# Index scores of a sparse attention layer: f32 products over half the rows replaced by pairs of F32R products over all 128

## The chip, the cores and the metric

The kernel runs on one core of a Trainium2 chip. The metric is the device time of one execution in microseconds; the figure given for a kernel is the median of several executions. Engines are named as the profile names them: PE multiplies matrices (PEld is its weight load), DVE is VectorE, ACT is ScalarE, POOL is GpSimd and SP issues most transfers.

## What is computed

Two blocks of two layers each, over 256 tokens (272 with 16 learned ones in the second block). The change sits in the third layer, whose first half is an attention in which every token attends only to the 64 keys with the highest index score:

```
iqb = iq[:, s0:s0 + 128]                                   # 8 index heads of 64
sc = jax.nn.relu(jnp.einsum('bqhd,bsd->bqhs', iqb, ik).astype(jnp.float32))
score = jnp.einsum('bqhs,bqh->bqs', sc, iwb.astype(jnp.float32)) * IDX_SCALE
score = jnp.where(adm[None], score, NEG_INF)
_, idx = lax.top_k(score, topk)                            # topk = 64
```

`iq` has 8 heads of 64, `ik` has one key of 64 for all heads, `iw` a weight for each head. `iq`, `ik` and `iw` are columns of one large input product of the layer.

## The kernel before

Activations lie transposed, features on partitions and tokens along the row. A large product is done in two parts: `hilo` (L338 to L341) writes a rounded copy of an f32 tile in the type F32R on ACT and the remainder, also F32R, on DVE, and `mm3` adds three products of such parts in one PSUM bank. `Stream.emit` (L267 to L293) loads each piece of weights (128x1024), splits it the same way (ACT at L289, DVE at L290) and keeps eight pieces; `take` hands two pieces to a product and asks for later ones, so L289 of a new piece has to wait until PE has read the piece that stood in its buffer. `tiles2` (L608) takes two pieces and makes two output tiles in the two PSUM banks `pd`, each from 24 matmuls of 272 columns; the next `tiles2` needs both banks evicted.

In `layer_ab` the input product gives, in this order: the tile `zn` with the index key, head weights and gate input; the four tiles `ps` with the index queries; `pq`; then by `tiles2` the GLA keys (evicted at L1251 into `k_`), two pairs of attention keys `ak` and two pairs of attention queries `aq` (all four pairs evicted at L1261 into the tile `akq`), and the values. While PE makes these, DVE, ACT and PE also do `decays` (L1333 to L1354: exponentials and cumulative sums of the gate) and `select`.

`select` evicts the four tiles of queries into the first half of `akq` (L1364), copies the key to both halves of the partitions (`ik`), and then, for each of two blocks of 128 queries (`wd` = 144 and 272 keys), makes eight score tiles in the four banks `pw`: one f32 matmul for each head, over 64 rows, two heads beside each other on the two halves of the rows. ACT takes relu from PSUM into `rl` (L1381, two buffers), and DVE adds them up with the head weight (L1383, L1385). Then DVE finds the 64 largest by eight rounds of `max` and `match_replace` (L1389, L1390).

The program is written in this order, but a scheduler of the framework sets the order of each engine's queue when the kernel is built, from its own estimates of times and from the buffers that come free. At run time every engine works through its queue in that order.

Of the kernel before, what the change touches and what calls it, by code (L numbers as in the profile page):

```python
# [10 lines left out]
F32 = mybir.dt.float32  # L11
F32R = mybir.dt.float32r
AF = mybir.ActivationFunctionType
OP = mybir.AluOpType
# [4 lines left out]
SEQ = 256  # L19
META = 16  # L20
T2 = SEQ + META
# [285 lines left out]
HALVES = slice(0, 64), slice(64, 128)  # L307


class K:  # L310
# [898 lines left out]
    def layer_ab(self, xh, xl, x, g):  # L1209

        nc, tc = self.nc, self.tc
        with tc.tile_pool(name="ab", bufs=1) as lp, tc.tile_pool(name="ab2", bufs=2) as l2:
# [6 lines left out]
            mk = [tile([128, wd], f"sc{t}") for t, wd in ((0, 144), (1, 272))]  # L1219

            w = [self.st.take() for _ in range(2)]
            zn = self.psum("w")[:, :T2]
            ps = [self.psum(b)[:, :SEQ] for b in "ddww"]
# [8 lines left out]
            _, r = self.lead(([[(zn, True)], [(ps[0], True), (ps[1], True)]], w), rest, hx, lx, T2)  # L1232
# [2 lines left out]
            nc.vector.tensor_scalar(rq, r, -0.125, None, op0=OP.mult)  # L1235
            nz = tile([128, T2], "nz")
            nc.vector.tensor_tensor(nz, zn, r, op=OP.mult)
            akq, gs = self.ag("akq", F32), self.ag("gs", F32)
            aq, ak = akq[:, :4], akq[:, 4:]
            eb, en, ed, qg = [gs[:, 2 * n:2 * n + 2] for n in range(4)]  # L1240
            dec = self.decays(nz, eb, en, ed, lp)
            self.select(nz, ps, r, mk, aq, lp, l2)

            kg, kdt = lp.tile([128, 2, T2], F32, tag="bc", name="kg"), tile([128, 3, 256], "kdt")
            for j, p in enumerate(pq):
# [27 lines left out]
            with tc.tile_pool(name="dsa", bufs=2) as dp:  # L1273
# [25 lines left out]
                ps = [self.psum("w")[:, :T2] for _ in range(4)]  # L1299
# [57 lines left out]
    def select(self, nz, ps, r, mk, iq, gp, l2):  # L1357

        nc = self.nc
        ik = gp.tile([128, T2], F32, name="ik")  # L1360
        nc.gpsimd.tensor_copy(ik[0:64], nz[0:64])
        nc.gpsimd.tensor_copy(ik[64:128], nz[0:64])
        for j in range(4):
            nc.vector.tensor_tensor(iq[:, j, 16:], ps[j], r[:, 16:], op=OP.mult)  # L1364
        iw = gp.tile([128, 2, 8], F32, name="iw")
        p = self.psum("m")
        for t in range(2):
            nc.tensor.transpose(p[:, 8 * t:8 * t + 8], nz[64:72, 16 + 128 * t:144 + 128 * t], self.ident[64:72, 64:72])
        nc.vector.tensor_scalar(iw.rearrange("p a b -> p (a b)"), p[:, :16], 64 ** -0.5 * 8 ** -0.5, None,
                                op0=OP.mult)  # L1370
        for t, sc in enumerate(mk):
            wd = sc.shape[1]
            for h in range(8):

                if h % 2 == 0:
                    two = [self.psum("w")[:, :wd] for _ in range(2)]
                    for p, hs in zip(two, HALVES):
                        self.mm(p, iq[hs, h // 2, 16 + 128 * t:144 + 128 * t], ik[hs, :wd])
                p = two[h % 2]
                rl = l2.tile([128, T2], F32, tag="rl", name="rl")[:, :wd]  # L1380
                nc.scalar.activation(rl, p, AF.Relu)  # L1381
                if h == 0:
                    nc.vector.tensor_scalar(sc, rl, iw[:, t, 0:1], None, op0=OP.mult)  # L1383
                else:
                    nc.vector.scalar_tensor_tensor(sc, rl, iw[:, t, h:h + 1], sc, op0=OP.mult, op1=OP.add)  # L1385
            nc.vector.memset(sc[0:64, wd - 64:wd], -BIG)
            m8 = gp.tile([128, 8], F32, name=f"m8{t}")
            for _ in range(8):
                nc.vector.max(m8, sc)  # L1389
                nc.vector.match_replace(sc, m8, sc, -3e38)  # L1390
            nc.vector.tensor_scalar(sc, sc, -2e38, BIG, op0=OP.is_gt, op1=OP.mult)
# [524 lines left out]
```

## Time and profile before

| | |
|---|---|
| median of 3 runs | 986.51 us (984.84 to 987.99) |
| the profiled execution | 982.69 us, span 980.9 us |
| PE busy | 956.9 us, 98% of the span |
| DVE busy | 667.9 us, 68% |
| ACT busy | 515.9 us, 53% |
| POOL busy | 92.0 us, 9% |
| mean granted clock of PE | 0.992 |

The span is the time from the first to the last instruction of the program in the one execution that was profiled; 1.8 us of that execution lie outside it. PE's busy time is modelled at its end, so a matmul's listed duration is longer than the distance to the next one; where rates are needed, distances between starts are read.

### The profile page before, as it was taken

Reading aid. Unit: us, or ns where it says so; the run is one execution under the profiler, and the core shown is the slowest. Engines: PE = TensorE matmul, PEld = TensorE weight load, DVE = VectorE, ACT = ScalarE, POOL = GpSimd, SP = SyncE. Lnnn points to the kernel's source line nnn. Section 1 sums busy time; section 2 is a strip of 40 time slices with the busy share of each in tenths; the row PEclk is TensorE's granted clock in tenths of the full one; section 3 lists DMA queues with packets and bytes.
Section 4 is the critical chain, followed back from the end, with each engine's and each line's share of the span. In section 5 each row is a group of like instructions: output and inputs, shape, how many; then the busy total and the mean of one; then the engine's idle time right before and its main releaser. Section 6 shows DMA issues by size and latency. Waiting matters only on the chain.

```text
span 980.9 us, 19189 instructions
## 1 busy us (share of the span) xinstructions
PE 956.9 (98%) x7638; PEld 898.9 (92%) x7638; DVE 667.9 (68%) x1369; ACT 515.9 (53%) x933; POOL 92.0 (9%) x121
## 2 busy tenths in 40 slices
PE   7999999999999999999999999999999999999996
PEld 6999989999999898887999999989898889998985
DVE  6889577545554899984954555558987756757762
ACT  7646366444445568873734444445635435353442
POOL 1121010000001100001000000010211211005121
PEclk9999999999999999999999999989999999999999
DMA  9744437655554364421565555546354314634201
GB/s 330 269 158 146 141 125 263 203 184 172 177 192 150 122 219 136 156 80 45 175 217 191 173 173 192 190 145 231 108 178 147 119 45 131 234 130 130 88 1 44
DMA packets 46074, 154.65 MB, mean 158 GB/s; under 512 B 6424, under 2 KB 7968, under 8 KB 45856
## 3 DMA queue, kind: packets, MB, share of 16 engines
q1 hardware_dynamic: 45552, 152.85, 46.5%
q8 instruction: 60, 0.98, 0.4%
q10 hardware_dynamic: 432, 0.57, 0.2%
q14 instruction: 30, 0.25, 0.1%
HBM read 152.34 MB, written 2.70 MB: 158 GB/s over the span
## 4 chain that ended last, share of the span: by engine, by line
PE 93%; DVE 3%; ACT 1%; DMA 1%; issue 1%; POOL 1%; SPq 0%; POOLq 0%; DVEq 0%; ACTq 0%
PE pd L328 45%; PE pw L328 38%; PE pm L328 6%; DVE st L290 1%; PE pm L1140 1%; PE pm L1172 1%; DMA st<-in_c_v 1%; DMA x<-in_xT 1%; ACT pm L1126 0%; POOL rc L389 0%; DVE zz L1030 0%; PE pm L1528 0%; PE pm L1730 0%; DVE x L521 0%; PE pw L881 0%
## 5 line engine op out<-in xcount | busy, mean ns | idle before, releaser
L290 DVE TENSOR_TENSOR st<-st,st 128x1024 fp32r<-128x1024 f32 (+2 forms) x274 | 327.3, 1212 | 162.7 <-ACT st L289 162.0
L289 ACT ACTIVATE st<-st 128x1024 fp32r<-128x1024 f32 (+2 forms) x274 | 279.4, 1041 | 275.1 <-PE pd L328 140.9
L328 PE MATMUL pd<-xh,st 128*128 128x256 f32 (+1 forms) x1856 | 357.0, 287 | 8.3 <-ACT st L289 6.3
L328 PEld LDWEIGHTS pd<-xh,st 128*128 128x128 f32 x1856 | 293.4, 189 | 15.5 <-ACT st L289 6.3
L328 PE MATMUL pd<-xl,st 128*128 128x256 f32 (+1 forms) x928 | 263.9, 286 | 0.6 <-DVE xl L428 0.6
L328 PE MATMUL pw<-hh,st 128*128 128x256 f32 x1024 | 188.4, 283 | 0.0
L328 PEld LDWEIGHTS pd<-xl,st 128*128 128x128 f32 x928 | 175.7, 189 | 2.8 <-DVE xl L428 1.3
L328 PEld LDWEIGHTS pw<-hh,st 128*128 128x128 f32 x1024 | 161.1, 191 | 0.0
L328 PE MATMUL pw<-hl,st 128*128 128x256 f32 x512 | 144.6, 283 | 0.0
L328 PEld LDWEIGHTS pw<-hl,st 128*128 128x128 f32 x512 | 98.0, 191 | 0.0
L328 PE MATMUL pd<-akq,st 128*128 128x272 f32 (+1 forms) x384 | 78.0, 293 | 0.0
L328 PE MATMUL pw<-xh,st 128*128 128x256 f32 (+1 forms) x384 | 75.2, 286 | 0.0
L328 PEld LDWEIGHTS pd<-akq,st 128*128 128x128 f32 x384 | 61.0, 188 | 2.3 <-issue 1.9
L328 PEld LDWEIGHTS pw<-xh,st 128*128 128x128 f32 x384 | 61.3, 190 | 1.1 <-ACT xh L533 0.7
L328 PE MATMUL pd<-gs,st 128*128 128x272 f32 (+1 forms) x192 | 55.3, 288 | 0.0
L328 PE MATMUL pw<-xl,st 128*128 128x256 f32 (+1 forms) x192 | 54.1, 284 | 0.0
L389 POOL TENSOR_TENSOR rc<-rc,mhalf 128x2 f32<-128x2 f32 (+4 forms) x17 | 19.9, 1173 | 317.6 <-DVE rc L386 314.6
L328 PE MATMUL pw<-mh,st 128*128 128x256 f32 x256 | 48.7, 285 | 0.3 <-ACT mh L340 0.2
L328 PEld LDWEIGHTS pw<-mh,st 128*128 128x128 f32 x256 | 40.3, 190 | 1.7 <-ACT mh L340 0.6
L328 PEld LDWEIGHTS pd<-gs,st 128*128 128x128 f32 x192 | 36.2, 189 | 0.5 <-issue 0.4
L328 PEld LDWEIGHTS pw<-xl,st 128*128 128x128 f32 x192 | 36.3, 189 | 0.0
L328 PE MATMUL pw<-ml,st 128*128 128x256 f32 x128 | 36.1, 289 | 0.0
(457 smaller groups left out, 1321.6 us busy)
## 6 DMA issues: line engine op xcount, KB each, us to landing
st<-in_w SPq DMA_DIRECT2D x128, 512.0 KB, 4.5
st<-in_ab_in SPq DMA_DIRECT2D x32, 512.0 KB, 3.9
st<-in_cd_in SPq DMA_DIRECT2D x28, 512.0 KB, 4.3
st<-in_a_in SPq DMA_DIRECT2D x18, 512.0 KB, 7.0
st<-in_c_in SPq DMA_DIRECT2D x16, 512.0 KB, 4.7
st<-in_a_out SPq DMA_DIRECT2D x8, 512.0 KB, 4.7
st<-in_c_out SPq DMA_DIRECT2D x8, 512.0 KB, 4.1
st<-in_ab_out SPq DMA_DIRECT2D x8, 512.0 KB, 3.9
```

The costliest lines, as they stand in the source:

```text
L289: self.last = self.nc.scalar.activation(hi[:, p], raw[:, p], AF.Copy).ins
L290: self.nc.vector.tensor_tensor(lo[:, p], raw[:, p], hi[:, p].bitcast(F32), op=OP.subtract)
L328: self.pe = self.nc.tensor.matmul(out, lhsT, rhs, start=start, stop=stop, skip_group_check=True).ins
L389: nc.gpsimd.tensor_tensor(r, r, self.mhalf[:p, :n], op=OP.pow)
L1140: nc.tensor.transpose(tp[:, 128 * j:128 * j + 128], src, self.ident)
L1172: nc.tensor.transpose(ps[:b - a, 128 * j:128 * j + 128], x[:, a:b], self.ident)
```

## The change

`select` now splits the index key and the index queries into F32R parts. The key's rounded part `ikh` and remainder `ikl` both stand on both halves of the rows (L340, L341). Each head of the queries gets a tile of all 128 rows: its rounded part on the half where the head came out of the product (ACT, L1373), the remainder on the other half (DVE, L1374, from the f32 copy `iqf` of L1371). One matmul with `ikh` and one with `ikl` then add all four products of parts in one bank. The eight heads fill the whole tile `akq`, so `layer_ab` asks for that tile a second time, for `aq` and `ak`, after `select`: the buffer is the same one, and its first writer (L1263) waits for the last index matmul.

```
@@ layer_ab
-            akq, gs = self.ag("akq", F32), self.ag("gs", F32)
-            aq, ak = akq[:, :4], akq[:, 4:]
+            iq, gs = self.ag("akq", F32R), self.ag("gs", F32)
             eb, en, ed, qg = [gs[:, 2 * n:2 * n + 2] for n in range(4)]
             dec = self.decays(nz, eb, en, ed, lp)
-            self.select(nz, ps, r, mk, aq, lp, l2)
+            self.select(nz, ps, r, mk, iq, lp, l2)
+            akq = self.ag("akq", F32)
+            aq, ak = akq[:, :4], akq[:, 4:]
@@ select
+        ikh, ikl = gp.tile([128, T2], F32R, name="ikh"), gp.tile([128, T2], F32R, name="ikl")
+        self.hilo(ikh, ikl, ik)
         for j in range(4):
-            nc.vector.tensor_tensor(iq[:, j, 16:], ps[j], r[:, 16:], op=OP.mult)
+            q = l2.tile([128, T2], F32, tag=f"vf{j % 2}", name="iqf")[:, :SEQ]
+            nc.vector.tensor_tensor(q, ps[j], r[:, 16:], op=OP.mult)
+            for f, h in enumerate(HALVES):
+                nc.scalar.activation(iq[h, 2 * j + f, :SEQ], q[h], AF.Copy)
+                nc.vector.tensor_tensor(iq[HALVES[1 - f], 2 * j + f, :SEQ], q[h], iq[h, 2 * j + f, :SEQ].bitcast(F32),
+                                        op=OP.subtract)
...
             for h in range(8):
-
-                if h % 2 == 0:
-                    two = [self.psum("w")[:, :wd] for _ in range(2)]
-                    for p, hs in zip(two, HALVES):
-                        self.mm(p, iq[hs, h // 2, 16 + 128 * t:144 + 128 * t], ik[hs, :wd])
-                p = two[h % 2]
+                p = self.psum("w")[:, :wd]
+                self.mm(p, iq[:, h, 128 * t:128 * t + 128], ikh[:, :wd], True, False)
+                self.mm(p, iq[:, h, 128 * t:128 * t + 128], ikl[:, :wd], False, True)
```

The scheduler orders the queues anew. Three places show it. The first is PE's queue where the third pair of `tiles2` begins (`pd_8469` before, `pd_8510` now: the second pair of attention keys). Before, the index matmuls of the second block stand one or two at a time between the projection's:

```order
L328 MATMUL pd_8469<-xl_7723,st1_8310 128x272
L328 MATMUL pw_8264<-ik_8173,akq_8135 128x272
L328 MATMUL pd_8469<-xh_7722,st2_8311 128x272
L328 MATMUL pd_8469<-xh_7722,st1_8310 128x272
L328 MATMUL pd_8469<-xl_7723,st1_8310 128x272
L328 MATMUL pd_8469<-xh_7722,st2_8311 128x272
L328 MATMUL pd_8470<-xh_7722,st1_8316 128x272
L328 MATMUL pd_8470<-xl_7723,st1_8316 128x272
L328 MATMUL pd_8470<-xh_7722,st2_8317 128x272
L328 MATMUL pw_8265<-ik_8173,akq_8135 128x272
L328 MATMUL pw_8274<-ik_8173,akq_8135 128x272
```

Now all sixteen of the second block, and the last four of the first, stand in one row ahead of that pair (its end is shown; `pw_8276` is the first of them, and each needs the bank of the head four before it):

```order
L328 MATMUL pw_8294<-ikh_8176,akq_8135 128x272
L328 MATMUL pw_8294<-ikl_8177,akq_8135 128x272
L328 MATMUL pw_8300<-ikh_8176,akq_8135 128x272
L328 MATMUL pw_8300<-ikl_8177,akq_8135 128x272
L328 MATMUL pw_8306<-ikh_8176,akq_8135 128x272
L328 MATMUL pw_8306<-ikl_8177,akq_8135 128x272
L328 MATMUL pw_8312<-ikh_8176,akq_8135 128x272
L328 MATMUL pw_8312<-ikl_8177,akq_8135 128x272
L328 MATMUL pw_8318<-ikh_8176,akq_8135 128x272
L328 MATMUL pw_8318<-ikl_8177,akq_8135 128x272
L328 MATMUL pd_8510<-xh_7722,st1_8351 128x272
L328 MATMUL pd_8510<-xl_7723,st1_8351 128x272
```

What was strewn among the projections' matmuls is now one block between the second and the third of these pairs.

The second place is ACT's queue from the last weight piece before `select` on. Before (L1381 is relu, L1335 to L1343 belong to `decays`):

```order
L289 ACTIVATE st_8400<-st_8399 128x1024
L289 ACTIVATE st_8458<-st_8457 128x1024
L1381 ACTIVATE rl<-pw 128x144 x2
L1335 ACTIVATE gs<-gs 128x544
L1381 ACTIVATE rl<-pw 128x144 x2
L1336 ACT_TABLE_LOAD
L1336 ACTIVATE gs<-gs 128x544
L289 ACTIVATE st_8464<-st_8463 128x1024
L1381 ACTIVATE rl<-pw 128x144 x3
```

Now (L1389 is relu, L1337 to L1345 belong to `decays`, `st_8441`, `st_8499`, `st_8505` and `st_8563` are the pieces 8400, 8458, 8464 and 8522 of before):

```order
L289 ACTIVATE st_8441<-st_8440 128x1024
L1373 ACTIVATE akq<-iqf 64x256 x8
L340 ACTIVATE ikh<-ik 128x272
L289 ACTIVATE st_8499<-st_8498 128x1024
L289 ACTIVATE st_8505<-st_8504 128x1024
L1389 ACTIVATE rl<-pw 128x144 x2
L289 ACTIVATE st_8563<-st_8562 128x1024
L1337 ACTIVATE gs<-gs 128x544
L1389 ACTIVATE rl<-pw 128x144 x2
L1338 ACT_TABLE_LOAD
L1338 ACTIVATE gs<-gs 128x544
L1389 ACTIVATE rl<-pw 128x144
```

Nine copies came in, and two weight pieces that stood behind the first relus now stand ahead of them or among them.

The third place is DVE's queue around the first evictions of attention keys. Before, the first stands nine rows further ahead, among the first block's sums; the second stands here, ahead of the second block's first sum (`sc_7901` and `sc_7902` are the score tiles of the two blocks):

```order
L290 TENSOR_TENSOR st_8523<-st_8521,st_8522 128x1024
L1385 SCALAR_TENSOR_TENSOR sc_7901<-rl,iw,sc_7901 128x144 x2
L1261 TENSOR_TENSOR akq<-pd,r 128x272
L1386 MEMSET sc_7901 64x64
L1383 TENSOR_SCALAR sc_7902<-rl,iw 128x272
```

Now both stand behind the fifth sum of the second block:

```order
L1393 SCALAR_TENSOR_TENSOR sc_7902<-rl,iw,sc_7902 128x272
L1397 MAX m_8258<-sc_7901 128x8
L1393 SCALAR_TENSOR_TENSOR sc_7902<-rl,iw,sc_7902 128x272
L1398 MATCH_REPLACE sc_7901<-m_8258,sc_7901 128x144
L1393 SCALAR_TENSOR_TENSOR sc_7902<-rl,iw,sc_7902 128x272
L1263 TENSOR_TENSOR akq<-pd,r 128x272 x2
```

The two evictions free the `pd` banks that the third pair needs.

## Rows read from the trace of the kernel before

**Rows 1.** The page: engines (busy us, share, instructions), chain that ended last.

```profile
PE 956.9 (98%) x7638; PEld 898.9 (92%) x7638; DVE 667.9 (68%) x1369; ACT 515.9 (53%) x933; POOL 92.0 (9%) x121
...
PE 93%; DVE 3%; ACT 1%; DMA 1%; issue 1%; POOL 1%; SPq 0%; POOLq 0%; DVEq 0%; ACTq 0%
```

**Rows 2.** Busy time by window (us: PE, PEld, DVE, ACT, POOL, PEclk, DMA, GB/s).

```profile
678.00:712.00 34.00, 34.00 (x228) 28.43 (x227) 29.19 (x84) 18.40 (x32) 6.30 (x8) 1.00 0.42 147
```

**Rows 3.** Timeline of PE (start, us, what, count): index matmuls among projections; each leaves two records.

```profile
682.89 0.28 PE L328 MATMUL pd<-xl,st 128*128 128x272 f32 x1
683.10 0.51 PE L328 MATMUL pw<-ik,akq 64*128 64x144 f32 x2
683.54 0.52 PE L328 MATMUL pd<-xh,st 128*128 128x272 f32 x2
683.90 0.29 PE L328 MATMUL pd<-xl,st 128*128 128x272 f32 x1
...
694.25 0.73 PE L328 MATMUL pw<-ik,akq 64*128 64x272 f32 x4
694.90 0.40 PE L328 MATMUL pd<-xl,st 128*128 128x272 f32 x1
...
696.27 0.29 PE L328 MATMUL pd<-xh,st 128*128 128x272 f32 x1
696.49 0.72 PE L328 MATMUL pw<-ik,akq 64*128 64x272 f32 x2
697.14 0.39 PE L328 MATMUL pd<-xh,st 128*128 128x272 f32 x1
697.37 0.29 PE L328 MATMUL pd<-xl,st 128*128 128x272 f32 x1
```

**Rows 4.** Timeline of DVE in the same stretch (idle before in brackets).

```profile
680.50 1.23 DVE L290 TENSOR_TENSOR st<-st,st 128x1024 fp32r<-128x1024 f32 x1
681.64 0.50 DVE L1333 TENSOR_SCALAR gs<-pm,ab_s 128x272 f32<-128x272 f32 x1
683.97 0.44 DVE L1251 TENSOR_TENSOR k__8371<-pd,r 128x272 f32<-128x272 f32 x1 [1.84 <-PE pd L328]
...
693.23 1.73 DVE L1340 TENSOR_TENSOR_SCAN bc<-one,gs 128x16 f32<-128x16 f32 x10
...
702.51 0.49 DVE L1385 SCALAR_TENSOR_TENSOR sc<-rl,iw,sc 128x272 f32<-128x272 f32 x1
```

**Rows 5.** Timeline of ACT in the same stretch.

```profile
683.26 1.06 ACT L289 ACTIVATE st<-st 128x1024 fp32r<-128x1024 f32 x1 [2.79 <-PE pd L328]
...
688.38 0.48 ACT L1381 ACTIVATE rl<-pw 128x144 f32<-128x144 f32 x2
688.88 1.28 ACT L1336 ACT_TABLE_LOAD   x1
690.17 0.66 ACT L1336 ACTIVATE gs<-gs 128x544 f32<-128x544 f32 x1
690.73 1.05 ACT L289 ACTIVATE st<-st 128x1024 fp32r<-128x1024 f32 x1
```

**Rows 6.** Instructions of the tile akq elsewhere (ns min/median/max, first and last start us).

```profile
L340 ACT ACTIVATE akq<-mix x8: 399/409/422, 947.6 to 961.6; 128x256 fp32r<-128x256 f32 x8
L341 DVE TENSOR_TENSOR gs<-mix,akq x8: 411/414/789, 949.6 to 962.1; 128x256 fp32r<-128x256 f32 x8
```

**Rows 7.** Windows around two falls of the granted clock (columns as in rows 2).

```profile
320.70:324.10 3.40, 3.16 (x9) 2.25 (x10) 1.92 (x6) 0.64 (x2) 0.17 (x1) 0.50 0.50 154
...
648.90:651.70 2.80, 2.28 (x17) 1.80 (x15) 1.96 (x5) 1.52 (x3) 1.05 (x1) 1.00 0.41 103
651.80:658.60 6.80, 6.56 (x20) 4.34 (x21) 4.46 (x13) 2.04 (x4) 0.48 (x1) 0.50 0.53 160
```

**Rows 8.** Timeline of PE where it works densely again after those two falls.

```profile
323.86 0.61 PE L328 MATMUL pd<-xh,st 128*128 128x256 f32 x2
...
656.39 0.59 PE L328 MATMUL pw<-xh,st 128*128 128x272 f32 x1
```

## The prediction, made before the changed kernel ran

> **What bounds the kernel now.** I began with the engines' shares and the chain that ended last [rows 1]: PE is busy for 98% of the span and makes up 93% of the chain. Then I took the stretch of the change, 678 to 712 us [rows 2]: PE is busy in all 34 of 34 us at a granted clock of 1.00, DVE in 29.2, ACT in 18.4. So a microsecond of PE's work that goes is worth a microsecond, and DVE has less than 5 us of slack in these 34. Last I read the queues there, row by row, since new work on DVE and ACT counts only where PE waits for it.
>
> **What is removed.** An F32R matmul of 272 columns follows the last one by 0.126 us: from 682.89 to 683.90 stand three starts beside a stop, and without stops the rows advance so. The price of a stop for index scores is the distance over it, less what the projection matmuls in between would take. One head of 144 keys: 683.90 - 682.89 - 3 x 0.126 = 0.63 us. One head of 272 keys: 697.37 - 696.27 - 2 x 0.126 = 0.85 us. A pair of heads on both halves, at 694.25, holds PE for 0.65 us until the next start, and the single head at 696.49 for 0.65 as well [rows 3]: the second of a pair is free. The sixteen heads make eleven stops: three single ones, a pair, and one of three heads in the first block, two pairs and four single ones in the second. The third head of three I estimate at 0.24: a single head of 144 columns holds PE for 0.44 us (683.10 to 683.54) and one of 272 for 0.65, so 128 columns take 0.21 and 144 take 0.24. That is 4 x 0.63 + 0.87 + 6 x 0.85 = 8.5 us.
>
> The Trainium skill, TensorEngine Tiling (Array Packing), Row Tiling and Theoretical Speedup, says that a contraction of 64 rows or fewer lets two tiles of the array work at once, for up to twice the speed, which speaks against giving up the halves. If all heads went in pairs, as that rule has it, the old form would cost 4 x 0.63 + 4 x 0.85 = 5.9 us. The rows show pairs at one price, but most heads alone; so I keep 8.5, and by the rule the change would come out 2.6 us dearer.
>
> **What PE gets.** Thirty-two F32R matmuls. Sixteen of 272 columns at 0.126 are 2.0 us. Of 144 columns the trace has no F32R matmul. Lower bound: in proportion, 16 x 0.07 = 1.1 us. Upper bound: the f32 rate at the same width, 16 x 0.24 = 3.8 us. Neither is nearer, one by type, the other by width. Not all of the difference counts, since some of it falls into the wait below: I take 1.1 here and 0.7 for the rest, with 0 and 1.3 as ends. So PE's own work falls by 8.5 - 3.1 = 5.4 us.
>
> **What DVE and ACT get.** Nine copies on ACT; the nearest form, 128x256 from f32 to F32R, lasts 0.41 us, and the remainder on DVE 0.41 too [rows 6]. An instruction starts 0.09 before the one ahead of it is listed as ended (680.50 + 1.23 against 681.64 [rows 4]), so nine of them advance by some 0.33 each: 3 us on each engine. The f32 queries (L1371) replace L1364 in the same shape. Half as many partitions could make a copy cheaper, at most to nothing; the order of the queues, which costs more, would stay. On ACT the copies fall in idle time, the 2.79 us ahead of the piece at 683.26 [rows 5]. On DVE 1.84 us of waiting at 683.97 cover part, so the first GLA key is evicted about 1.2 us late; PE does not need that bank before 688. These additions are therefore nothing by themselves. If that cover were gone they would cost the 1.2 us.
>
> **The new wait.** I walk through the new queues with the old durations, from 681.6, up to which they agree.
> The second GLA product ends on PE at about 687.7. ACT's next weight piece, now ahead of all relus, waits for that (as the piece at 683.26 waited for PE [rows 5]); the piece takes 0.96 to the next start, and relus 0 and 1 end at 689.1. The next piece, again ahead of relus 2 and 3, waits for the end of the third product, 691.0. Then: piece 0.96, exponential 0.57, two relus, table load 1.28, logarithm 0.57 [rows 5], relu 4: 695.1. Another piece: relu 5 ends at 696.3. A second table load and two exponentials stand before relu 6, and they wait for DVE's sums over the gate (1.73 us [rows 4]), which wait for the logarithm: 699.1. Before relu 7 stands the last exponential of the gate, whose input DVE writes behind a weight remainder (1.14 from 680.50 to 681.64 [rows 4]): 701.1.
> PE ends the fourth product and the last heads of the first block at 694.7. The eight heads of the second block follow in one row, and each needs the bank whose relu was just timed: 695.2, 696.4, 699.2, 701.2. The others follow at the pace of relu and sum until 703.3. Behind them in the queue stands the third pair of projections, which needs a `pd` bank; the eviction that frees it stands behind DVE's fifth sum of the second block. From 701.5 five sums at 0.41 [rows 4] with two `max` and two `match_replace` between them end at 704.4, the eviction at 704.8. PE goes on at about 704.8 instead of 694.7 + 2.0 = 696.7: **8.1 us of waiting**. Two later evictions behind the `max` rounds add 0.6. Nothing hides this: every matmul of the layer is queued behind it, and nothing later in this layer waits for DVE long enough to give it back.
>
> **The clock.** PE would do 2 us of work in 10. Twice in this trace its clock fell to half, 1.2 GHz, after a thin stretch: after 648.90 to 651.70, in which PE has 17 matmuls, it stood at 0.50 for 6.8 us, and once, at 320.7, for 3.4 [rows 7]. What that costs is half of the dense work done before it rises. After the fall at 320.7 dense work began at 323.9 and the clock was back at 324.1: 0.1 us. After 651.8 it began at 656.4, and the clock was back by 658.6: 1.1 us [rows 8]. At most a fall of 6.8 us lies wholly over dense work, 3.4 us. I take 1.1.
>
> **Sum.** -5.4 + 8.1 + 0.6 + 1.1 + 0.7 = +5.1 us. The profiled execution took 982.69 us, so 987.8; it is 3.8 us below the median of the runs, 986.51. Against that median: **991.6 us**. A change of under 0.3%, 3 us, is what a measurement of this kernel can hardly tell from none.
>
> **Rivals.**
> - *The wait is short and the saving remains.* It ends on the other side if DVE reaches the eviction before PE has waited 5.4 us, so before about 702. The relus need 0.3 us and the sums 0.41 each; were it not for the weight pieces and the gate's exponentials queued between, they would keep up, as they do now while PE never waits. Against it: the order of the queues is fixed, and four separate waits would all have to shrink. With no wait left the time is 986.5 - 5.4 = 981.1.
> - *The wait is as forecast, but the clock stays up and 144 columns go at full rate.* Then +3.3 us: 989.8; with one or two of the waits shorter by 2 us, 988. For it: PE does not rest in one piece, and each wait is under 3 us.
> - *Clock down over dense work and 144 columns at the f32 rate.* 3.3 + 3.4 + 1.3 = +8.0: 994.5. For it: the projections that follow are dense at once.
> - *The first product with the new parts waits too*, for the remainder of the key on DVE (685.5 in the walk, while PE needs it at 687.7). Were the split operations half as long again, it would just begin to count; +1 us at most: 992.6. It lies within the forecast.
>
> **Chances.** Forecast with the last rival, +3 to +7 us: 0.60. Small loss, 0 to +3: 0.20. Both bad ends, over +7: 0.12. Short wait, a gain: 0.08, of which 0.06 are over 3 us. Around 3 us some of the forecast's lower part would be measured as no change, and as much of the small loss as slower, so slower 0.73, same 0.21, faster 0.06. The range runs from the small loss, +0.5, to the far end of the third rival, +9.5 with some scatter of the runs: 987.0 to 996.0. It leaves out the gain and the extremes.
>
> **What would show it.** Right: in PE's timeline a run of 20 index matmuls after the fourth projection with waits of 1 to 3 us between them, released by ACT's relu, then a wait for DVE's eviction of the first attention key; 8 to 9 us in all; a granted clock below 1 in one window from about 696 to 710; stops of F32R matmuls that add only their own columns. The step on 144 columns is wrong if their starts lie 0.07 apart or 0.24. The forecast is wrong if PE never waits over 1 us there, if relu 6 comes before 697, or if a later stretch of the layer takes back what was lost.

## The result, and the profile of the changed kernel

The changed kernel takes 990.43 us (median of 17 runs, 988.43 to 993.32), the kernel before, run beside it, 984.95 us (17 runs). The ratio is 1.0058, with a 95% interval of 1.0049 to 1.0068: 5.7 us slower, 4.8 to 6.7. The profiled execution has a span of 988.3 us at a mean granted clock of 0.988.

The page of the changed kernel, its engines and its chain, against [rows 1]:

```profile
PE 956.2 (97%) x7638; PEld 901.8 (91%) x7638; DVE 671.0 (68%) x1378; ACT 520.4 (53%) x942; POOL 93.8 (9%) x121
...
PE 89%; DVE 5%; ACT 2%; issue 1%; DMA 1%; POOL 1%; SPq 0%; POOLq 0%; DVEq 0%; ACTq 0%
```

PE's busy time hardly falls, although it has less work now (a matmul at half clock, see below, counts longer); its share of the chain falls from 93% to 89%, and DVE and ACT gain most of what it lost. So PE now waits for them. The windows of the stage (columns as in rows 2) say where:

```profile
692.00:696.00 4.00, 4.00 (x35) 4.00 (x34) 2.65 (x5) 2.98 (x5) 0.00 (x0) 1.00 0.67 218
696.00:700.00 4.00, 1.93 (x12) 1.33 (x11) 3.03 (x16) 3.96 (x7) 0.00 (x0) 1.00 0.40 131
700.00:704.00 4.00, 1.11 (x4) 0.80 (x4) 3.79 (x11) 2.36 (x7) 3.53 (x3) 0.80 0.29 77
704.00:708.00 4.00, 3.44 (x10) 2.00 (x8) 3.97 (x13) 2.23 (x6) 1.16 (x2) 0.50 0.14 56
708.00:712.00 4.00, 3.45 (x15) 3.45 (x16) 4.00 (x15) 0.80 (x2) 1.40 (x2) 0.50 0.01 2
712.00:716.00 4.00, 4.00 (x32) 3.96 (x31) 4.00 (x20) 1.44 (x2) 0.14 (x1) 0.92 0.01 4
```

Where PE was busy throughout in [rows 2], it is idle for 2.1 us of the second window and 2.9 us of the third, and from 702.4 to 712.6 its granted clock is 0.50, 1.2 GHz. PE's timeline, from the first gate product of the stage on:

```profile
680.98 0.69 PE L328 MATMUL pm<-nz,ab_s 16*128 16x272 f32 x2
...
696.61 0.28 PE L328 MATMUL pw<-ikl,akq 128*128 128x144 f32 x1
697.16 0.39 PE L328 MATMUL pw<-ikh,akq 128*128 128x272 f32 x1 [0.28 <-ACT rl L1389]
...
698.40 0.39 PE L328 MATMUL pw<-ikh,akq 128*128 128x272 f32 x1 [0.72 <-ACT rl L1389]
...
701.10 0.39 PE L328 MATMUL pw<-ikh,akq 128*128 128x272 f32 x1 [2.17 <-ACT rl L1389]
...
703.40 0.60 PE L328 MATMUL pw<-ikh,akq 128*128 128x272 f32 x1 [1.79 <-ACT rl L1389]
...
704.29 0.59 PE L328 MATMUL pw<-ikh,akq 128*128 128x272 f32 x1
...
706.69 0.59 PE L328 MATMUL pw<-ikh,akq 128*128 128x272 f32 x1
...
708.55 0.59 PE L328 MATMUL pd<-xh,st 128*128 128x272 f32 x1 [1.04 <-DVE akq L1263]
```

The eight heads of the second block stand in one row. The first four wait 5.0 us for ACT's relu in all, the next four come 0.8 us apart, and the third pair of projections waits for the eviction at L1263. What ACT does between these relus:

```profile
696.84 0.27 ACT L1389 ACTIVATE rl<-pw 128x144 f32<-128x144 f32 x1
697.01 1.05 ACT L289 ACTIVATE st<-st 128x1024 fp32r<-128x1024 f32 x1
698.06 0.29 ACT L1389 ACTIVATE rl<-pw 128x144 f32<-128x144 f32 x1
...
700.23 0.64 ACT L1346 ACTIVATE gs<-bc 128x544 f32<-128x544 f32 x1
700.77 0.27 ACT L1389 ACTIVATE rl<-pw 128x144 f32<-128x144 f32 x1
702.08 0.66 ACT L1355 ACTIVATE gs<-gs 128x544 f32<-128x544 f32 x1 [1.03 <-DVE gs L1351]
...
703.06 0.29 ACT L1389 ACTIVATE rl<-pw 128x144 f32<-128x144 f32 x1
```

A weight piece, the gate's exponentials and a wait for DVE stand between four relus of the first block, as the walk had them.

And DVE: its split work, and the eviction for which PE waits, behind a sum:

```profile
684.42 3.58 DVE L1374 TENSOR_TENSOR akq<-iqf,akq 64x256 fp32r<-64x256 f32 x8
...
707.65 0.49 DVE L1393 SCALAR_TENSOR_TENSOR sc<-rl,iw,sc 128x272 f32<-128x272 f32 x1
708.06 0.78 DVE L1263 TENSOR_TENSOR akq<-pd,r 128x272 f32<-128x272 f32 x2
```

### The profile page after: what moved, and what is told of

The parts are those of the page before. It is cut to its first block, busy times and chain, and to the rows that moved or that the text cites. A ratio compares the mean times of both kernels' runs of the same rounds, so it can differ in the third digit from the quotient of the medians.

```text
span 988.3 us, 19215 instructions
## 1 busy us (share of the span) xinstructions
PE 956.2 (97%) x7638; PEld 901.8 (91%) x7638; DVE 671.0 (68%) x1378; ACT 520.4 (53%) x942; POOL 93.8 (9%) x121
## 4 chain that ended last, share of the span: by engine, by line
PE 89%; DVE 5%; ACT 2%; issue 1%; DMA 1%; POOL 1%; SPq 0%; POOLq 0%; DVEq 0%; ACTq 0%
PE pd L328 43%; PE pw L328 37%; PE pm L328 6%; DVE st L290 1%; PE pm L1140 1%; DVE x L521 1%; PE pm L1172 1%; DMA st<-in_c_in 1%; DMA x<-in_xT 1%; ACT pm L1126 0%; POOL rc L389 0%; DVE sc L1393 0%; DVE zz L1030 0%; ACT st L289 0%; PE pm L1536 0%
```

## The experiments

Theory: the loss is PE waiting in a row of index matmuls that the shared buffer `akq` forces, with a fall of the clock on top; PE's own work did become shorter. Rivals: the 32 new matmuls are dear (144 columns above all); the split work on DVE and ACT holds PE up.

The profiled executions differ ahead of this stage already: its first gate product (`pm<-nz,ab_s` on PE, at 680.98 above) starts between 678.55 and 683.00 us. (PE waits 0 to 1.9 us just ahead of it for `nz`; the last seven DVE instructions up to `nz` are the same, in the same order, in all twelve profiles, so I put that wait down to the execution and not to the edit.) For the profiles I therefore give the time from that start to the end of the span as well. It is 980.9 - 679.37 = 301.5 us in the kernel before, and 988.3 - 680.98 = 307.3 us, 5.8 more, in the changed one. Ratios are to the kernel before, run on the same chip.

| kernel | median, us | ratio (95% interval) | start, span | stage to end, against before |
|---|---|---|---|---|
| changed | 990.43 | 1.0058 (1.0049 to 1.0068) | 680.98, 988.3 | +5.8 |
| changed, run again | 989.19 | 1.0058 (1.0043 to 1.0073) | 680.67, 987.5 | +5.3 |
| own buffer for the split queries | 979.63 | 0.9956 (0.9942 to 0.9969) | 679.92, 977.3 | -4.1 |
| before, with the shared buffer | 988.08 | 1.0049 (1.0034 to 1.0065) | 681.72, 985.9 | +2.6 |
| before, with the split work | 985.31 | 1.0021 (1.0009 to 1.0032) | 678.95, 983.3 | +2.8 |
| changed, waits filled | 988.15 | 1.0045 (1.0030 to 1.0060) | 678.55, 984.7 | +4.6 |
| changed, no low product | 989.30 | 1.0058 (1.0045 to 1.0070) | 678.83, 986.1 | +5.7 |
| own buffer, no low product | 979.00 | 0.9957 (0.9942 to 0.9972) | 681.91, 978.1 | -5.3 |
| own buffer, 80 more matmuls | 987.89 | 1.0042 (1.0030 to 1.0054) | 680.99, 985.6 | +3.1 |
| changed, no table loads | 989.21 | 1.0063 (1.0046 to 1.0080) | 680.54, 986.2 | +4.1 |
| waits filled, no table loads | 988.87 | 1.0052 (1.0039 to 1.0066) | 683.00, 987.7 | +3.2 |

### A buffer of its own for the split queries

```
-            iq, gs = self.ag("akq", F32R), self.ag("gs", F32)
+            gs = self.ag("gs", F32)
...
-            self.select(nz, ps, r, mk, iq, lp, l2)
+            with tc.tile_pool(name="iqp", bufs=1) as ip:
+                iq = ip.tile([128, 8, SEQ], F32R, name="iq")
+                self.select(nz, ps, r, mk, iq, lp, l2)
```

The pool is closed after `select`, so that a later pool reuses its 8 KB of each partition.

> The changed kernel with a buffer of its own for the split queries, so that the evictions of the attention keys and queries need not wait for the last index matmul. Theory (the lost time is PE waiting in one row of index matmuls that the shared buffer forces): the index matmuls stand apart again between projection matmuls, no wait over 1 us in the stage, granted clock 1.0 throughout; PE's own work is 8.5 us of stops less 32 F32R matmuls at 0.10 to 0.126 us, 3.6 us, so 4 to 6 us below the kernel before: 979 to 981 us, ratio 0.994 to 0.996. Rival A (the 32 matmuls over 128 rows are themselves dear): no better than the kernel before, 985 or more, with starts of index matmuls 0.2 us apart or more. Rival B (the split work on ACT and DVE holds PE up): 985 to 990, with PE waiting for DVE evictions elsewhere in the stage.

Measured: 979.63 us, 4.3 us faster than the kernel before (3.1 to 5.7), as expected, and the fastest kernel here that does the whole work. One window of 30 us (columns as in rows 2), and PE's rows at the end of the first block and the one wait of the stage:

```profile
682.00:712.00 30.00, 29.45 (x231) 28.56 (x230) 27.24 (x69) 18.90 (x36) 5.92 (x7) 1.00 0.44 139
```

```profile
696.24 0.27 PE L328 MATMUL pw<-ikl,iq 128*128 128x144 f32 x1
696.35 0.28 PE L328 MATMUL pw<-ikh,iq 128*128 128x144 f32 x1
696.46 0.27 PE L328 MATMUL pw<-ikl,iq 128*128 128x144 f32 x1
...
697.37 0.29 PE L328 MATMUL pw<-ikh,iq 128*128 128x272 f32 x1
697.50 0.29 PE L328 MATMUL pw<-ikl,iq 128*128 128x272 f32 x1
697.62 0.29 PE L328 MATMUL pd<-xl,st 128*128 128x272 f32 x1
...
703.23 0.39 PE L328 MATMUL pd<-xh,st 128*128 128x272 f32 x1 [0.55 <-DVE akq L1265]
```

The heads stand among projections again, a head of 272 keys takes 697.62 - 697.37 = 0.25 us without any stop around it, and the clock does not fall in the stage. Both rivals said that such a kernel could not be faster than before; they fall as causes of the loss. The same two edits (form of the product, buffer) make four kernels: in the shared buffer the new form is worth nothing, in its own buffer 4.3 us.

### The shared buffer alone, with f32 products

```
-            akq, gs = self.ag("akq", F32), self.ag("gs", F32)
-            aq, ak = akq[:, :4], akq[:, 4:]
+            iq, gs = self.ag("akq", F32), self.ag("gs", F32)
...
-            self.select(nz, ps, r, mk, aq, lp, l2)
+            self.select(nz, ps, r, mk, iq, lp, l2)
+            akq = self.ag("akq", F32)
+            aq, ak = akq[:, :4], akq[:, 4:]
```

> The kernel before with one edit of the change alone: the index queries take the whole buffer, and the attention queries and keys get it after the last index product; products stay f32 on half the rows, no split. Theory: the order becomes a row of five heads at the end of the index products with a wait of 2 to 4 us for relu, sum and eviction, while three stops of 0.85 us fall away: 0 to 2 us slower than before, less than the changed kernel loses, since here 11 of the 16 heads still stand apart. Rival (sharing the buffer alone costs all that the change lost): 5 us slower, ratio 1.005.

Measured: 4.8 us slower (3.3 to 6.4), where I had expected 0 to 2. PE's waits, and the window in which the clock was down:

```profile
702.38 1.01 PE L328 MATMUL pw<-ik,akq 64*128 64x272 f32 x4 [0.51 <-ACT rl L1382]
705.07 0.72 PE L328 MATMUL pw<-ik,akq 64*128 64x272 f32 x2 [1.68 <-ACT rl L1382]
706.52 0.60 PE L328 MATMUL pd<-xh,st 128*128 128x272 f32 x1 [0.73 <-DVE akq L1262]
```

```profile
706.00:709.40 3.40, 2.88 (x12) 2.88 (x13) 3.40 (x11) 1.13 (x3) 0.77 (x1) 0.50 0.19 70
```

The waits, 2.9 us, are as large as I said; I had left out that the clock would fall here too, over 2.9 us of PE's work, which costs up to 1.4 us. So the old products lose time as soon as they share the buffer. How much is less sure: the profiled execution shows +2.6, the runs at least 3.3.

### The split work alone, with f32 products

```
             nc.vector.tensor_tensor(iq[:, j, 16:], ps[j], r[:, 16:], op=OP.mult)
+            for f, h in enumerate(HALVES):
+                nc.scalar.activation(hq[h, 2 * j + f, :SEQ], iq[h, j, 16:], AF.Copy)
+                nc.vector.tensor_tensor(hq[HALVES[1 - f], 2 * j + f, :SEQ], iq[h, j, 16:], hq[h, 2 * j + f, :SEQ].bitcast(F32),
+                                        op=OP.subtract)
```

The key's two parts are made as well.

> The kernel before with the split work of the change alone: the nine copies on ACT and nine remainders on DVE are made into tiles that nothing reads, products stay f32. The schedule moves index heads to 13 stops in place of 11, which by itself is worth 1.7 us. Forecast (split work is covered by idle time of ACT and DVE): 1 to 3 us slower, no PE wait over 1 us. Rival (7 us more of DVE work, at 0.45 us for each remainder as the trace of the changed kernel has them, makes DVE late for PE): 4 us slower or more, with PE waits behind DVE evictions.

Measured: 2.1 us slower (0.9 to 3.1), within the expectation of 1 to 3. The split work itself, and the window over the stage:

```profile
L1369 ACT ACTIVATE hq<-akq x8: 414/416/420, 679.2 to 682.3; 64x256 fp32r<-64x256 f32 x8
L1370 DVE TENSOR_TENSOR hq<-akq,hq x8: 418/420/421, 682.4 to 685.6; 64x256 fp32r<-64x256 f32 x8
```

```profile
682.00:712.00 30.00, 30.00 (x189) 24.17 (x188) 26.78 (x71) 17.59 (x34) 6.76 (x8) 1.00 0.43 137
```

PE is busy in all 30 us, so nothing waits for the split work there. (The one wait of PE nearby, 1.0 us up to 678.95, ends ahead of the first copy.) The two stops more are one of 144 keys and one of 272, so 0.63 + 0.85 = 1.5 us by the prices of the forecast and not the 1.7 that I had expected; they cover most of the 2.1. (In this profile the clock stood at 0.50 from 801.7 to 805.1, past the attention, over dense work: up to 1.7 of the +2.8.)

### Matmuls into the waits, to keep the clock up

```
+                n = (0, 2, 14, 10, 2, 2, 2, 2)[h] if t else 0
+                for _ in range(n):
+                    with self.tc.issue_after(self.pe):
+                        self.mm(fill, ikh[:, :128], ikh)
```

> The changed kernel with 34 more F32R matmuls of 272 columns (4.3 us at full clock) into a bank that nothing reads, put between the heads of the second block, where PE waits: 2, 14 and 10 ahead of the second to fourth head and 2 ahead of each later one. They use waiting time, so the row's end is set by relu and sum as before. Theory (the fall of the clock is part of the loss, and it comes because PE is idle): granted clock stays near 1.0 from 696 to 712, and the time falls from 5.5 us above the kernel before to 2.5 to 3.5 above. If the fall is worth only the 1.1 us of the forecast: 4.4 above. Rival (the clock costs nothing here, or falls anyway): 5.5 above or more.

Measured: ratio 1.0045 where the changed kernel has 1.0058, so about 1.3 us less (the intervals overlap); in the profile 1.2 us less. That is 4.4 us above the kernel before (3.0 to 5.9), where the theory had 2.5 to 3.5. The windows up to the third pair and behind it:

```profile
694.70:705.70 11.00, 8.39 (x50) 6.64 (x50) 10.76 (x38) 7.44 (x15) 4.72 (x4) 1.00 0.24 79
705.70:712.00 6.30, 6.27 (x51) 6.21 (x51) 6.30 (x21) 1.80 (x3) 1.55 (x2) 1.00 0.02 4
```

The clock stays at 1.00 although PE still idles 2.6 us of the first 11; in the changed kernel it idles 5.1 of the 11 from 696.6 on. In all six runs the mean granted clock is 0.991 to 0.997, against 0.983 to 0.991 in the 23 runs of the changed kernel. So the clock does as the theory had it, and the time does not. In the changed kernel the dense work from 708.55 to 712.6 ran at half clock, which costs 2.0 us. That is what filling should give back; it gave 1.2. Part of the rest is visible later: the scheduler places the attention's small f32 products (64x16) in three rows here and in one in the changed kernel, where they cost PE less. The last four heads stand 0.8 us apart here too, so it is not the clock that spaces them.

### Less work for PE in the row, and less where it does not wait

```
-                self.mm(p, iq[:, h, 128 * t:128 * t + 128], ikh[:, :wd], True, False)
-                self.mm(p, iq[:, h, 128 * t:128 * t + 128], ikl[:, :wd], False, True)
+                self.mm(p, iq[:, h, 128 * t:128 * t + 128], ikh[:, :wd], True, True)
```

> The changed kernel without the second product of each index head (the low part of the keys is left out, so the scores are rounder): 16 of the 32 F32R index matmuls fall away, worth 8 x 0.11 + 8 x 0.126 = 1.9 us where PE is the bound. Theory (in the row of the changed kernel PE waits for relu, sums and the eviction, so its own work there is free): 0 to 0.8 us faster than the changed kernel, so still 4.7 us or more above the kernel before. Rival (the time of the changed kernel is PE's own new work): 1.9 us faster than the changed kernel, 3.6 above the kernel before.

> The same product left out of the kernel whose split queries have a buffer of their own, in which PE waited 0.5 us in all of the stage. Theory (there PE is the bound): the 1.9 us come off in full, so 1.5 to 2.2 us below that kernel, 6 to 7 below the kernel before, ratio 0.993 to 0.994. Rival (ACT and DVE bound that stage too): under 0.8 us below it.

In the shared buffer: 1.0058, exactly the changed kernel's ratio. Sixteen matmuls less gain nothing that the runs can show, and PE's waits for relus grow from 5.0 to 6.7 us (the view of waits: total, times, longest):

```profile
PE pw L328 <- ACT rl L1388: 6.7, 8, 2.3
```

In the own buffer my expectation failed: 0.9957 against 0.9956, no gain that the runs can show, and 1.2 of 1.9 us in the profile. The wait for L1265 grew there:

```profile
704.95 0.39 PE L328 MATMUL pd<-xh,st 128*128 128x272 f32 x1 [1.59 <-DVE akq L1265]
```

It had been 0.55 us, and 1.0 us more of it is enough for the rest. So in this profile PE is the bound of the stage only as long as about a microsecond of its work there is not taken away; then DVE's eviction comes too late.

### The price of 144 columns

```
+                for _ in range(0 if t else 10):
+                    self.mm(p, iq[:, h, 128 * t:128 * t + 128], ikl[:, :wd], False, False)
```

> The kernel with the own buffer and 80 more F32R matmuls of 144 columns: the low product of each head of the first block is done ten times more. What one costs: 0.107 us by the starts in the trace of that kernel (from 696.24 to 696.46 stand two steps of 0.11), 0.07 if columns alone counted, 0.24 at the f32 rate of the forecast's upper bound. So 8.6 us, 5.6 us or 19 us more than that kernel, less up to 1 us of waiting that the longer rows cover; the starts within a row of 11 show it directly.

Measured: 1.0042 against 0.9956, 8.5 us more, as expected (7.2 in the profile). A row of one product with `ikh` and eleven with `ikl`, and the start of the next:

```profile
694.32 0.28 PE L328 MATMUL pw<-ikh,iq 128*128 128x144 f32 x1
694.44 1.39 PE L328 MATMUL pw<-ikl,iq 128*128 128x144 f32 x11
695.66 0.28 PE L328 MATMUL pw<-ikh,iq 128*128 128x144 f32 x1
```

Twelve take 1.34 us, 0.11 each: neither 0.07 nor 0.24.

### No table loads between the relus

```
-        nc.scalar.activation(la, la, AF.Exp)
-        nc.scalar.activation(la, la, AF.Ln, bias=1.0)
+        nc.scalar.activation(la, la, AF.Copy)
+        nc.scalar.activation(la, la, AF.Copy)
```

The four exponentials behind them become copies too.

> The changed kernel with the gate's exponentials and logarithm replaced by copies of the same shape (the gate's values are then not the reference's), so that ACT loads no function table twice, 1.28 us each, between the relus. Theory (relus 4 to 7 come late because they stand behind the table loads and the gate's chain on ACT): the waits of PE for relus shrink by 2 to 2.6 us in all, the third pair of projections begins that much earlier, and the time falls by 1.5 to 2.6 us below the changed kernel, to 3 to 4 us above the kernel before. Rival (the row is paced by DVE or by PE itself): less than 0.8 us below the changed kernel.

> The kernel with matmuls in its waits and, on top, the gate's exponentials and logarithm as copies (the gate's values are then not the reference's). All queues keep their order but for the two table loads on ACT that go. The row without table loads began its third pair of projections 1.4 us earlier, counted from the last pair of heads of the first block, yet its median did not fall; there the clock stood at half over 3.4 us of dense work. Theory (the table loads hold up relus, and so PE, and the clock hid it or the scatter of the runs did): with the clock kept up, 1.2 to 2 us below the kernel with the filled waits, so 2.4 to 3.2 us above the kernel before. Rival (the table loads cost nothing in the end, since something later takes it up): within 0.5 us of the filled kernel, 4 to 5 above the kernel before.

> The changed kernel itself, unaltered, on the same chip as the run beside it, as the level to compare with: 5 to 6 us above the kernel before, ratio 1.005 to 1.0065. If it came out under 1.004, the differences of 1 us between the forms of the row could not be told apart.

The last head of the first block and the third pair of projections, with no table loads:

```profile
696.17 0.28 PE L328 MATMUL pw<-ikl,akq 128*128 128x144 f32 x1
...
706.68 0.59 PE L328 MATMUL pd<-xh,st 128*128 128x272 f32 x1 [1.04 <-DVE akq L1263]
```

That is 10.5 us, against 708.55 - 696.61 = 11.9 in the changed kernel: the row is 1.4 us shorter, and from the stage to the end both profiles without table loads are shorter than their counterparts, by 1.7 (+4.1 against +5.8) and 1.4 (+3.2 against +4.6). The waits for relus fall from 5.0 to 3.8 us, where 2 to 2.6 less were expected. The medians do not follow: 1.0063 beside 1.0058, and 1.0052 beside the 1.0045 of the filled kernel. Both expectations failed by that, and the times are as the rivals had them, or a little longer. The changed kernel run again gave 1.0058 once more, as expected. The table loads do stand in PE's way in the two executions that were profiled; whether a run is shorter without them stays open, as the intervals are 2 to 3 us wide and I found no place later in the traces that takes the time back.

## Why the prediction was right, and where its sizes were off

**The direction and the cause.** The forecast was 991.6, 5.1 us above the 986.51 it started from, with slower as the likeliest, by a wait that takes the place of the stops. The measured 5.7 us and the run with the own buffer, 10 us faster than the changed kernel with the same matmuls, show that the cause is the buffer's second use and the wait behind it. In the trace stand the signs that were named: twenty index matmuls in a row after the fourth projection (696.32 to 707.08), relus that release PE after up to 2.2 us (two of the four waits are under 1 us), the eviction at L1263 behind them, and one stretch of low clock, though from 702.4 on and not from 696. The sizes below were off by more than the total shows; that they nearly cancel is luck.

**PE's own work.** The sum had -5.4 + 0.7 = -4.7 us. With the own buffer the stage is 4.1 us shorter and holds 0.55 us of waiting: -4.7. Of the two estimates inside it, that for 144 columns was 1.1 + 0.7 = 1.8 us, and 16 x 0.11 = 1.8 was measured; that leaves about the 8.5 us of the sum for the stops, which no run measured alone. The half between the bounds that I took was luck rather than insight.

The Trainium skill, TensorEngine Tiling (Array Packing), Row Tiling and Theoretical Speedup, was weighed against this: had the heads of the old form gone in pairs, as the rule has it, the new form would gain 2.6 us less, 1.6 with the own buffer. The run gained 4.3 (3.1 to 5.7), so the rows decide: seven of the eleven stops were single heads, and a lone head costs a whole stop. ("Most heads alone" in the forecast is true of the stops only; of the sixteen heads, seven stood alone.)

**The walk through the queues.** From the first gate product (679.37 before, 680.98 after) to the last head of the first block the walk had 694.7 - 679.4 = 15.3 us; the trace has 696.72 - 680.98 = 15.7. To the third pair it had 704.8 - 679.4 = 25.4; the trace has 27.6. So the wait is 27.6 - 15.7 - 2.0 = 9.8 us instead of **8.1**. Relus 5 to 7 ended 0.3 to 0.6 us later than walked. The rest came behind them: I let the last heads follow at 0.41 us for a sum, but relu waits for DVE to free one of its two buffers, and DVE runs a `max` or a `match_replace` between two sums, so the heads come 0.8 us apart. In the trace of the changed kernel:

```profile
704.63 0.40 ACT L1389 ACTIVATE rl<-pw 128x272 f32<-128x272 f32 x1 [0.39 <-DVE sc L1393]
...
706.34 0.49 DVE L1393 SCALAR_TENSOR_TENSOR sc<-rl,iw,sc 128x272 f32<-128x272 f32 x1
706.75 0.30 DVE L1397 MAX8 m<-sc 128x8 f32<-128x144 f32 x1
706.97 0.48 DVE L1393 SCALAR_TENSOR_TENSOR sc<-rl,iw,sc 128x272 f32<-128x272 f32 x1
```

**The clock** was mis-sized: 1.1 us taken, 2.0 on the trace, since dense work began at 708.55 and the clock was back only at 712.6. It stayed inside the bound of 3.4. With the waits filled, so that PE idles 2.6 us and not 5.1, the clock does not fall, so PE's idling is what brings it down here. The forecast counted two falls in the trace of the kernel before; there is a third, from 976.0 to the end of the span, in which PE does nothing.

**Later evictions** were put at +0.6. No such wait is in the trace. Instead something is given back: -4.7 + 9.8 + 2.0 is +7.1, and the stage to the end shows +5.8. Most of the 1.3 us stands in the attention that follows, whose f32 products the scheduler also placed anew. The small ones (64x16), in four rows before (717.56, 720.91, 727.26, 741.91), now stand in one:

```profile
749.59 1.27 PE L328 MATMUL pw<-akq 64*16 64x16 f32 x24
750.79 0.39 PE L328 MATMUL pd<-xh,st 128*128 128x272 f32 x1
```

Its 24 records take 1.20 us. In the kernel before the three small rows cost 0.35 each, priced as the forecast priced a stop (717.94 - 717.34 - 2 x 0.126), and the large one 1.09, so 2.1 in all: 0.9 us less now. The wide ones (64x144 and 64x272) took 0.90, 0.65, 0.44 and 0.90 us in four rows before (from 749.21, 757.64, 767.46 and 768.37); now three rows (from 757.00, 764.97 and 775.10) take 0.45, 0.66 and 0.90, another 0.9 us less. The first of them, before (upper line) and now:

```profile
749.21 0.97 PE L328 MATMUL pw<-akq 64*128 64x144 f32 x6
757.00 0.52 PE L328 MATMUL pw<-akq 64*128 64x144 f32 x4
```

Against that, a row of other products behind them takes 9.1 us (784.69 to 793.81) where it took 8.4 (777.97 to 786.37), 0.7 more. Together that is 1.1 of the 1.3 us; why the scheduler placed them so was not tested. The errors of the forecast are +1.7, +0.9 and -1.9.

**Split work as nothing by itself** held, though each operation advances by 0.43 to 0.45 us and not by 0.33 (eight copies 3.49 us, eight remainders 3.58), and the first GLA key was evicted 2.8 us later, not 1.2 (688.39 - 680.98 against 683.97 - 679.37). PE did not wait for it, so the rival in which the first product waits for the key's remainder fell too.

**The other rivals.** The short wait falls with 5.0 + 1.0 us of waits in the trace, and the clock that stays up with the window at 0.50. Of the third rival the clock over dense work came true in part (2.0 of 3.4 us), the f32 rate for 144 columns did not (0.11 against 0.24).

## What to carry to other kernels

Before a tile is given a second use, look who else waits for its first one: a buffer saved can turn work that stood spread among dense matmuls into one row whose every step waits for another engine. Here a buffer of its own is worth 10 us and makes the same change a gain. Where an engine waits in a row, its own work there is free: here sixteen matmuls less gained nothing, and 34 more cost nothing. So a faster operation must be judged together with the order that it gets.

## What the runs showed that was not expected

An F32R matmul of 144 columns takes 0.11 us, one of 272 columns 0.126: between these two widths the time hardly follows the columns. The Trainium skill, TensorE: Matmul & The Clock Gate, LDWEIGHTS (loading the stationary operand), gives a weight load as the number of weight columns divided by 1.2, in ns; by that formula 128 columns take an estimated 107 ns. Each of these matmuls loads 128 columns of weights; the trace lists such a load at 0.19 us, but the loads start 0.11 us apart, and that step agrees with the formula. No run here changed the weights' columns of these matmuls, so that they are the reason is not shown.

A copy or a remainder over 64 partitions and 256 elements takes 0.42 us on ACT and DVE, no less than the 0.41 over 128 partitions [rows 6]; halving the partitions saves nothing.
